# A two-layer decoder trunk in float32: layer B projects keys, queries, values in this order, with the norm gains in the weights, the branch shares in halves and the output projection in three passes

## The chip, the cores and the metric

The kernel runs on one NeuronCore of a Trainium2 chip. The metric is device time in microseconds (us) of one execution; before the change it was measured three times, with a median of 1330.33 us (1330.18 to 1332.09).

## The reference

The sequence has S = 512 tokens of D = 1024 channels, in float32; a head has 64 channels. Layer A is a sparse attention beside a memory attention, followed by a squared-relu MLP. Layer B, which the change is about, reads keys and values that are computed once from layer A's output. Cut to that part:

```
# layer A has left x; layer B:
k_s, v_s = split(rmsnorm(x, kv_norm) @ w_kv_shared, 2)      # 1024 -> 512 + 512, eight slots of 64
k = rope(rmsnorm(heads(k_s), kv_k_norm), pos);  v = heads(v_s)
h = rmsnorm(x, attn_norm[1])
q, q_mem = split(h @ b_w_in, [1536])                        # three groups of eight heads, four memory heads
q = rope(rmsnorm(q, b_q_norm), pos)
for gi, (window, dil) in enumerate(((128, 1), (512, 4), (2048, 16))):
    s = q[gi] . k[t - dil * j] / 8,  j = 0 .. window // dil # only t - dil * j >= 0
    lse[gi] = logsumexp(s);  out[gi] = softmax(s) . v
o_main = sum(out * softmax(lse over the three groups))
o_mem  = memory_attention(q_mem, mem_kv)                    # 256 memory rows, four heads
x = x + concat(o_main, o_mem) @ b_w_out                     # 768 -> 1024
x = x + squared_relu(rmsnorm(x, mlp_norm[1]) @ w_up) @ w_down
```

## The kernel before

**Number format.** Every float32 operand of a large product is kept as a high part, rounded to the format that TensorE reads, and a low part, the rest. A product is three matmuls: high by high, high by low, low by high (`mm3`, L232 to L234). For a weight, `wload` issues a DMA into a staging tile `s_st` (pool of three), ScalarE (ACT) writes the high part (`wsplit`, L225), and VectorE (DVE) or GpSimd (POOL) subtracts it for the low part (L227); the letters in `lo` choose between the two, "v" and "g". An activation is split in the same way; where a norm's gain belongs to it, `part` scales by the gain column while it splits (ACT L248, DVE L249).

**Order of the work.** The program is written as generators which are stepped against each other: `attend` walks through the attention items, and after each front (scores and exponentials) or back (the product with the values) it steps a side queue once and the list `work` as often as the ratio `RB` of that segment says. That fixes buffers and waits; a scheduler then orders the instructions of every engine by a model of their durations, so what stands on PE is not the program's order word for word. All weight loads are issued by SP's queue in order.

**Layer B** (L1351 to L1410). The transposed activations `xk`, multiplied by the gain of the K/V norm, come out of the end of layer A's MLP (`gained`, L1117, called at L1188). Keys are projected from w_kv[0] into the PSUM pool `pS` (blocks 2, 3, 0, 1), normalised and rotated, on POOL mostly (rope L483 to L486, L1381). Then the values are projected from w_kv[1]; each block of them is written to memory by a DMA that POOL issues (L1363), since `keys_b` reads them back in other row orders (L1464, L1466). Then 16 `gained` parts make `xg`, the same activations with layer B's own norm gain. Then the queries of slot pair 0 (`proj_b(0)`, 96 matmuls of 384 columns; evacuation L1424, ropes L483 to L486, L658, splits L617/L618, transposes on PE L667) are weaved with `keys_b(0)` (L1455 gathers, L1432). After step 34 of these, two steps of `work` follow each step.

`attn_b` makes eight items for each of four slot pairs: two halves of the tokens (`ih`), two slots (`s`), and `w` = 0 for the two groups with regular rows (window 128 and dilation 4), `w` = 1 for dilation 16 (scores L1492, exponentials L1522, transposes L1540 and L1549, value products L1562 and L1575). `close0` and `close1` take the sums out of PSUM. `norm_b` (L1584 to L1641) then merges the branches: it turns the statistics of `w` = 0 into the row order of `w` = 1 (L1589, L1595), works out the share of each branch (L1600 to L1615), transposes the shares (L1619), spreads them over the channels with two selection matmuls (L1627, L1632), multiplies (L1630, L1633), adds on POOL (L1634), and casts and splits on DVE (L1638, L1639). It begins in the side queue after `close1`, and `NY`, `NZ` are the steps that it lets pass in between. `work` holds the projections and keys of slot pairs 1 to 3, the memory queries and keys, and `outpart(0,2)`, the output projection of the first two chunks of the contraction, which adds its PSUM to the residual (L1084). After the last item, `outpart(2,6)` does the other four.

The names in the profile: `s_w` weights, `s_act` activations, `s_acc`, `s_ps`, `s_pt`, `s_po` the four PSUM pools (2, 3, 2 and 1 banks), `s_qk` split queries and keys, `s_qki` their split before the transposes, `s_tq` queries under way, `s_nb` the shares.

Of the kernel before, what the change touches and what calls it, by code (L numbers as in the profile page):

```python
# [47 lines left out]
RB = (1.58, 1.85, 1.49, 2.67, 1.4)  # L48
# [4 lines left out]
WK = 0.12  # L53
WB = (34, 2)

DELAY = 5

NY, NZ = 6, 2
# [107 lines left out]
class K:  # L166
# [105 lines left out]
    def proj(self, xg, wsrc, n, evac, blocks=NB, per=2, stat=None, banks=None, pool=None, lo="v", fine=False, hook=None, order=None):  # L272
# [259 lines left out]
    def mem_q(self, l, xg, wsrc, e, res):  # L532
# [13 lines left out]
        yield from self.proj(xg, wsrc, 256, evac, per=4, lo="gv")  # L546
# [513 lines left out]
    def outpart(self, oT, k0, k1, wsrc, xsrc, w0):  # L1060
# [56 lines left out]
    def gained(self, dst, m, h, gname):  # L1117

        H = S // 2
        self.part(dst[:, :, h * H : h * H + H], self.xh[h][m // 2][:, m % 2], self.gcol(gname)[:, m : m + 1])  # L1120

    def mlp(self, l):
# [43 lines left out]
        def columns(rows, cols):  # L1166

            for i in range(2):
# [8 lines left out]
                t = self.xh[rows][mp] = self.t("x", [P, 2, H])  # L1177
# [173 lines left out]
    def layer_b(self):  # L1351
# [412 lines left out]
```

## Time and profile before

| | |
|---|---|
| median of three runs | 1330.33 us |
| the profiled execution | 1332.11 us |
| its span, first to last instruction | 1330.3 us |
| mean granted TensorE clock | 0.982 |
| PE busy | 1272.9 us, 6425 instructions |
| DVE, ACT, POOL busy | 952.9, 765.9, 559.6 us |
| layer B up to its MLP | about 704 to 1000 us of the span |

The span is cut into stages by what runs there. From 704 to 764 us stand the projections of keys, values and the first queries; from 764 to 800 the second queries and the keys of pair 0; from 800 to 922 the attention of most pairs with the other projections; from 922 to 970 the last pair's end and the memory attention; from 970 the last part of the output projection. A row with "<-" and a releaser at its end names what the instruction waited for, and how long.

### The profile page before, as it was taken

The numbers are of one execution on the slowest core, as the hardware profiler recorded it, in microseconds if no ns is written. First come the engines' busy times: TensorE is split into PE (matmuls) and PEld (weight loads), VectorE is DVE, ScalarE is ACT, GpSimd is POOL, SyncE is SP. The second block draws the span as 40 slices with busy tenths as digits, with TensorE's granted clock in tenths as the row PEclk, the third lists the DMA queues.
The fourth block names the chain that finished last, engine by engine and source line by source line (L and its number), as shares of the span: only waits on it lengthen the run. The fifth ranks groups of instructions, "written<-read, shape, count | busy, mean of one in ns | idle before, by whom it ended". The sixth has DMA issues, their size and how long they took to land.

```text
span 1330.3 us, 18523 instructions
## 1 busy us (share of the span) xinstructions
PE 1272.9 (96%) x6425; PEld 1039.0 (78%) x6425; DVE 952.9 (72%) x1645; ACT 765.9 (58%) x1742; POOL 559.6 (42%) x578
## 2 busy tenths in 40 slices
PE   8999999999999999999999989989899999999997
PEld 6777787777787888888877879877578788888886
DVE  5877677764669678696798476676658967769586
ACT  5657577773465454554557557776655546355462
POOL 3765475442155041341415697452416324133140
PEclk9999899999999999999999999999899999999999
DMA  8313111023522525325244321012232342624423
GB/s 302 104 57 98 63 49 40 4 70 97 156 92 77 179 80 174 127 92 162 96 139 135 123 84 62 23 33 84 72 119 95 112 149 88 188 97 126 144 80 111
DMA packets 51534, 139.11 MB, mean 105 GB/s; under 512 B 5648, under 2 KB 12816, under 8 KB 51440
## 3 DMA queue, kind: packets, MB, share of 16 engines
q1 hardware_dynamic: 50224, 134.66, 32.3%
q0 software_dynamic: 640, 2.21, 0.5%
q8 instruction: 51, 0.84, 0.3%
q10 hardware_dynamic: 576, 1.05, 0.2%
q14 instruction: 43, 0.35, 0.1%
HBM read 132.66 MB, written 5.24 MB: 104 GB/s over the span
## 4 chain that ended last, share of the span: by engine, by line
PE 71%; DVE 16%; ACT 6%; issue 3%; DMA 3%; POOL 0%; DVEq 0%; ACTq 0%; POOLq 0%
PE s_ps L233 11%; PE s_ps L234 11%; PE s_ps L232 11%; DVE s_w L227 6%; PE s_acc L233 5%; PE s_acc L232 5%; PE s_acc L234 5%; DVE s_p L1104 3%; PE s_po L1045 3%; PE s_pt L232 2%; PE s_pt L233 2%; PE s_pt L234 2%; ACT s_w L225 2%; PE s_pt L1032 1%; PE s_ps L996 1%
## 5 line engine op out<-in xcount | busy, mean ns | idle before, releaser
L227 DVE TENSOR_TENSOR s_w<-s_st,s_w 128x1024 fp32r<-128x1024 f32 (+3 forms) x168 | 203.5, 1214 | 163.8 <-ACT s_w L225 163.1
L225 ACT ACTIVATE s_w<-s_st 128x1024 fp32r<-128x1024 f32 (+3 forms) x200 | 188.3, 946 | 157.3 <-PE s_pt L234 31.8
L232 PE MATMUL s_ps<-s_act,s_w 128*128 128x512 f32 x600 | 235.1, 393 | 2.0 <-ACT s_act L267 1.4
L233 PE MATMUL s_ps<-s_act,s_w 128*128 128x512 f32 x600 | 234.4, 391 | 0.0
L234 PE MATMUL s_ps<-s_act,s_w 128*128 128x512 f32 x600 | 234.1, 391 | 0.0
L1090 POOL TENSOR_TENSOR s_x<-s_x,s_st 128x512 f32<-128x512 f32 x64 | 102.0, 1611 | 90.3 <-DVE s_w L227 90.3
L232 PEld LDWEIGHTS s_ps<-s_act,s_w 128*128 128x128 f32 x600 | 112.4, 188 | 28.0 <-ACT s_act L267 3.1
L233 PEld LDWEIGHTS s_ps<-s_act,s_w 128*128 128x128 f32 x600 | 112.7, 188 | 24.2 <-issue 0.8
L234 PEld LDWEIGHTS s_ps<-s_act,s_w 128*128 128x128 f32 x600 | 112.7, 188 | 23.9 <-POOL s_p L642 0.8
L1090 POOL TENSOR_TENSOR s_x<-s_qki,s_st 128x512 f32<-128x512 f32 x16 | 25.2, 1573 | 214.5 <-DMA s_st<-in_w_db_dram 194.8
L232 PE MATMUL s_acc<-s_w,s_act 128*128 128x512 f32 (+2 forms) x272 | 99.6, 371 | 11.5 <-ACT s_w L225 5.5
L642 POOL TENSOR_SCALAR s_p<-s_p,s_cr 128x256 f32<-128x256 f32 (+3 forms) x128 | 71.9, 576 | 86.8 <-DVE s_cr L1008 25.5
L233 PE MATMUL s_acc<-s_w,s_act 128*128 128x512 f32 (+2 forms) x272 | 98.9, 364 | 0.1
L234 PE MATMUL s_acc<-s_w,s_act 128*128 128x512 f32 (+2 forms) x272 | 97.1, 361 | 0.0
L227 DVE TENSOR_TENSOR s_w<-s_x,s_w 128x512 fp32r<-128x512 f32 x96 | 90.5, 978 | 8.1 <-ACT s_w L225 8.1
L227 POOL TENSOR_TENSOR s_w<-s_st,s_w 128x512 fp32r<-128x512 f32 (+3 forms) x32 | 55.2, 1727 | 81.5 <-ACT s_w L225 62.7
L267 ACT ACTIVATE s_qk<-s_p 128x256 fp32r<-128x256 f32 (+1 forms) x96 | 47.0, 490 | 64.0 <-DVE s_p L1104 62.0
L1219 ACT ACTIVATE s_p<-s_ps 128x512 f32<-128x512 f32 x64 | 38.0, 593 | 79.3 <-PE s_ps L234 79.3
L270 DVE TENSOR_TENSOR s_qk<-s_p,s_qk 128x256 fp32r<-128x256 f32 (+1 forms) x96 | 76.9, 801 | 8.0 <-ACT s_qk L267 8.0
L225 ACT ACTIVATE s_w<-s_x 128x512 fp32r<-128x512 f32 x96 | 57.2, 623 | 38.1 <-POOL s_x L1090 38.1
L232 PEld LDWEIGHTS s_acc<-s_w,s_act 128*128 128x128 f32 x272 | 53.2, 196 | 17.8 <-ACT s_w L225 5.5
L1104 DVE TENSOR_TENSOR s_p<-s_p,s_p 128x256 f32<-128x256 f32 x96 | 59.5, 620 | 3.9 <-ACT s_p L1220 3.9
(347 smaller groups left out, 3218.4 us busy)
## 6 DMA issues: line engine op xcount, KB each, us to landing
s_st<-in_w_db_dram SPq DMA_DIRECT2D x80, 512.0 KB, 3.6
s_st<-in_w_up_dram SPq DMA_DIRECT2D x64, 512.0 KB, 3.7
s_st<-in_w_bq_dram SPq DMA_DIRECT2D x16, 384.0 KB, 3.2
s_st<-in_w_ag_dram SPq DMA_DIRECT2D x11, 512.0 KB, 4.4
s_act<-in_w_c_dram SPq DMA_DIRECT2D x8, 512.0 KB, 5.1
s_st<-in_w_mem_dram SPq DMA_DIRECT2D x8, 512.0 KB, 3.5
s_st<-in_w_ao_dram SPq DMA_DIRECT2D x16, 256.0 KB, 2.6
s_tq<-in_w_db_dram SPq DMA_DIRECT2D x16, 256.0 KB, 3.1
```

The source lines that it names most:

```text
L225: nc.scalar.activation(w[:, 0], st, AF.Copy)
L227: e.tensor_tensor(out=w[:, 1], in0=st, in1=w[:, 0], op=ALU.subtract)
L232: mm(ps, lh[0], rh[0], start=start, stop=False, skip_group_check=again)
L233: mm(ps, lh[0], rh[1], start=False, stop=False, skip_group_check=again)
L234: mm(ps, lh[1], rh[0], start=False, stop=stop, skip_group_check=again)
L267: nc.scalar.activation(dst[:, 0], src, AF.Copy)
L270: nc.vector.tensor_tensor(out=dst[:, 1], in0=src, in1=dst[:, 0], op=ALU.subtract)
L642: self.nc.gpsimd.tensor_scalar(out=p, in0=p, scalar1=c, scalar2=1.0, op0=ALU.mult, op1=ALU.mult)
L1045: nc.tensor.matmul(O[x * 64 : x * 64 + 64, q0 + o : q0 + 256], v[:, j, br, :], st[x][br][:, j, o:256], start=half == 0 and br == 0 and j = ...
L1090: self.nc.gpsimd.tensor_tensor(out=o, in0=x, in1=b[:, i * 512 : (i + 1) * 512], op=ALU.add)
L1104: tt = lambda o, x, y, op: nc.vector.tensor_tensor(out=o, in0=x, in1=y, op=op)
L1219: nc.scalar.activation(u, ps, AF.Relu)
```

## The change

The three-matmul products and the total of matmuls remain. These things change:

- `wload` takes gains. The rows of w_kv, w_bq and w_bm are multiplied by the norm gain while they are split: per k-chunk one scaled copy on ACT (L252) and one DVE instruction (L253), in place of one ACT copy and one subtraction, on DVE or POOL in turn, over the whole load. `gained` goes away: the end of layer A's MLP splits the plain activations, and one set of them serves keys, values and all queries.
- The order is keys, queries of pair 0, values. Of `proj_b(0)` all 36 steps of matmuls come first, into `pS`; then the values, into `pacc`, are weaved with its late steps and with `keys_b(0)`. `keys_b` waits for the fourth block of values before it reads them back. The interleaving after step 34 (`WB`) is gone.
- `norm_b` becomes three: `turned_b` enters the side queue after the last front of `w` = 0, `shares_b` after the last front of `w` = 1, and `join_b` runs inside `close1`. The sum moves from POOL to DVE, the copy from DVE to ACT (L1655).
- The output projection gets a third pass: `outpart(2,3)` joins `work`, on `pacc`, and the last is `outpart(3,6)`. It evacuates eight blocks more.
- The ratios RB rise for pairs 0 to 2.

```
-RB = (1.58, 1.85, 1.49, 2.67, 1.4)
+RB = (2.3, 2.3, 2.3, 2.67, 1.4)
-WK = 0.12
-WB = (34, 2)
+WK = 0.4
-NY, NZ = 6, 2
+NY, NZ = 1, 1
...
+        n = src.shape[-1] // gains.shape[1]
+        for j in range(gains.shape[1]):
+            c = slice(j * n, (j + 1) * n)
+            self.part(w[:, :, c], st[:, c], gains[:, j : j + 1])
...
-                    self.gained(self.xk[m], m, rows, "kv")
+                    self.split(self.xk[m][:, :, rows * H : rows * H + H], t[:, m % 2])
...
-        drain(self.proj(xk, ins["w_kv"][0], 512, evac_k, pool=self.pS, order=(2, 3, 0, 1)))
-        drain(self.proj(xk, ins["w_kv"][1], 512, evac_v, pool=self.pS))
-        xg = [self.t("act", [P, 2, S], F32R) for _ in range(KT)]
-        for m in range(KT):
-            for h in range(2):
-                self.gained(xg[m], m, h, "attn1")
...
+        work.add(self.outpart(oT, 2, 3, ins["w_bo"], None, 2, self.pacc))
+        drain(self.proj(xg, ins["w_kv"][0], 512, evac_k, pool=self.pS, order=(2, 3, 0, 1), gain="kv"))
+        q0, k0 = self.proj_b(0, xg, e, pb[0], self.pS), self.keys_b(0, kn, vd, kp[0])
+        v0 = self.proj(xg, ins["w_kv"][1], 512, evac_v, gain="kv")
+        for _ in range(NB * (KT + 1)):
+            next(q0)
+        drain(weave(v0, chain(q0, k0), WK))
...
-        drain(self.outpart(oT + om, 2, 6, ins["w_bo"], None, 2))
+        drain(self.outpart(oT + om, 3, 6, ins["w_bo"], None, 3))
...
+        while self.vrows < NB:
+            yield
...
+            if s == 1 and ih == 1:
+                side.add(self.shares_b(st1, s0, acc) if w else self.turned_b(st0, s0))
...
-            side.add(self.norm_b(st0, st1, acc[0], O, oT))
+            while len(acc) < 2:
+                side.step()
+            self.join_b(acc, O, oT)
...
-        nc.gpsimd.tensor_tensor(out=acc, in0=acc, in1=cb, op=ALU.add)
+        nc.vector.tensor_tensor(out=acc, in0=acc, in1=cb, op=ALU.add)
-        nc.vector.tensor_copy(nat(o[:, 0, :]), ap)
+        nc.scalar.activation(nat(o[:, 0, :]), ap, AF.Copy)
```

Since lines are inserted, later lines carry other numbers after the change: the matmuls L232 to L234 become L236 to L238, L225 becomes L229, L667 becomes L673, L564 and L577 become L570 and L583, L617, L624, L625 and L650 become L623, L630, L631 and L656, L1575 becomes L1579, L1619 becomes L1630.

**First place: PE, behind the queries of pair 0.** Before the change, PE's rows at the end of these queries (`s_ps`) are followed by the second queries (`s_acc`); the L667 rows are the transposes of the first ones:

```order
L233 MATMUL s_ps_7615<-s_w_7448,s_act_7382 128x384
L234 MATMUL s_ps_7615<-s_w_7448,s_act_7382 128x384
L232 MATMUL s_acc_7667<-s_w_7659,s_act_7375 128x384
L232 MATMUL s_acc_7746<-s_w_7659,s_act_7375 128x384
L667 MATMUL s_pt_7506<-idr,s_qki_7482 128x128 x4
L667 MATMUL s_pt_7513<-idr,s_qki_7482 128x128 x2
L233 MATMUL s_acc_7667<-s_w_7659,s_act_7375 128x384
```

After it, the same transposes (`s_pt_7345`) stand within the projection of the values (`s_acc`, 512 columns), 25 matmuls behind the end of the queries:

```order
L238 MATMUL s_acc_7517<-s_w_7512,s_act_6779 128x512
L237 MATMUL s_acc_7559<-s_w_7512,s_act_6779 128x512
L238 MATMUL s_acc_7559<-s_w_7512,s_act_6779 128x512
L236 MATMUL s_acc_7517<-s_w_7526,s_act_6830 128x512
L673 MATMUL s_pt_7345<-idr,s_qki_7326 128x128 x4
L673 MATMUL s_pt_7352<-idr,s_qki_7326 128x128 x2
L237 MATMUL s_acc_7517<-s_w_7526,s_act_6830 128x512
```

What moved: the 96 matmuls of the values, which stood ahead of the queries, now stand between their last matmul and their last transposes (94 of the 96 are ahead of these), and the second queries begin behind the values.

**Second place: ACT, at the memory keys of the end stage.** Before, two weight copies (L225) stand near the evacuations of the memory queries' transposes (L673) and keys (L624, L625):

```order
L225 ACTIVATE s_w_10087<-s_st_10085 128x512
L1567 ACTIVATE s_raw_9481<-s_po_9472 128x512
L650 ACTIVATE s_pt_2096_9535<-s_pt_9592 128x256
L650 ACTIVATE s_pt_2116_9628<-s_pt_9629 128x256
L673 ACTIVATE s_qk_9214<-s_pt_9633 128x2x128
L673 ACTIVATE s_qk_9215<-s_pt_9633 128x2x128
L617 ACTIVATE s_qki_9657<-s_tq_9655 128x4x64
L225 ACTIVATE s_w_10106<-s_st_10104 128x512
L624 ACTIVATE s_qk_9641<-s_pt_9647 64x4x128
```

After, there are six of them (L229) in the same stretch, most of 128x128, the third pass's:

```order
L656 ACTIVATE s_pt_2096_9584<-s_pt_9626 128x256
L229 ACTIVATE s_w_10057<-s_st_10055 128x128
L229 ACTIVATE s_w_10073<-s_st_10071 128x128
L656 ACTIVATE s_pt_2117_9679<-s_pt_9680 128x256
L229 ACTIVATE s_w_10083<-s_st_10081 128x128
L229 ACTIVATE s_w_10108<-s_st_10106 128x128
L679 ACTIVATE s_qk_9260<-s_pt_9691 128x2x128
L679 ACTIVATE s_qk_9261<-s_pt_9691 128x2x128
L623 ACTIVATE s_qki_9715<-s_tq_9713 128x4x64
L229 ACTIVATE s_w_10125<-s_st_10123 128x128
L229 ACTIVATE s_w_10149<-s_st_10147 128x384
L630 ACTIVATE s_qk_9699<-s_pt_9705 64x4x128
```

What moved: the copies for the third pass, each behind a DMA of its own, now stand in ACT's queue ahead of the evacuations.

**Third place: PE, the same stretch.** Before, no projection matmul stands between the transposes of the last pair and of the memory queries:

```order
L667 MATMUL s_pt_9633<-idr,s_qki_9610 128x128 x4
L564 MATMUL s_pt_9647<-idr,s_qki_9644 128x128 x4
L1575 MATMUL s_po_9699<-s_pt_2116_9628,s_x_9212 64x128
L1575 MATMUL s_po_9699<-s_pt_2096_9535,s_x_9212 64x128
L1575 MATMUL s_po_9699<-s_pt_2116_9628,s_x_9212 64x128
L1575 MATMUL s_po_9699<-s_pt_2096_9535,s_x_9212 64x128
L564 MATMUL s_pt_9660<-idr,s_qki_9657 128x128 x4
L1549 MATMUL s_pt_9695<-c_101,s_p_2115_9624 128x128 x2
L577 MATMUL s_ps_9677<-s_qk_9640,s_qk_9214 128x256
```

After, the third pass's matmuls (into `s_acc` of 128x512, one chunk of the contraction each time) stand among the same transposes (L673, L570), and the transposes of the shares (L1630) are already there:

```order
L238 MATMUL s_acc_10035<-s_act_9328,s_w_10032 128x512
L1630 MATMUL s_pt_9684<-idr,s_nb_9676 8x128 x4
L673 MATMUL s_pt_9691<-idr,s_qki_9644 128x128 x4
L236 MATMUL s_acc_10060<-s_act_9328,s_w_10057 128x512
L237 MATMUL s_acc_10060<-s_act_9328,s_w_10057 128x512
L238 MATMUL s_acc_10060<-s_act_9328,s_w_10057 128x512
L570 MATMUL s_pt_9705<-idr,s_qki_9702 128x128 x4
L236 MATMUL s_acc_10076<-s_act_9328,s_w_10073 128x512
L237 MATMUL s_acc_10076<-s_act_9328,s_w_10073 128x512
L238 MATMUL s_acc_10076<-s_act_9328,s_w_10073 128x512
L570 MATMUL s_pt_9718<-idr,s_qki_9715 128x128 x4
```

What moved: 24 matmuls that stood behind everything, in the last part of the output projection, now lie between the small steps of the last pair.

More of the change, by code (lines that the diff above doesn't have):

```diff
@@ L270, in split, with proj @@
         nc.vector.tensor_tensor(out=dst[:, 1], in0=src, in1=dst[:, 0], op=ALU.subtract)
-    def proj(self, xg, wsrc, n, evac, blocks=NB, per=2, stat=None, banks=None, pool=None, lo="v", fine=False, hook=None, order=None):
+    def proj(self, xg, wsrc, n, evac, blocks=NB, per=2, stat=None, banks=None, pool=None, lo="v", fine=False, hook=None, order=None, gain=None):
         ws = []
@@ L325, in proj @@
                     while len(ws) < min(nw, k // per + 2):
-                        ws.append(self.wload(wsrc[len(ws)], lo[len(ws) % len(lo)]))
+                        i = len(ws) * per
+                        gs = self.gcol(gain)[:, i : i + per] if gain else None
+                        ws.append(self.wload(wsrc[len(ws)], lo[len(ws) % len(lo)], gs))
                 if ps is None:
@@ L530, in mem_kv, with mem_q @@
         res.append(kf)
-    def mem_q(self, l, xg, wsrc, e, res):
+    def mem_q(self, l, xg, wsrc, e, res, gain=None):
         nc = self.nc
@@ L544, in evac @@
             return self.q_out(G, f, [q4[0][:, :, blk], q4[1][:, :, blk]])
-        yield from self.proj(xg, wsrc, 256, evac, per=4, lo="gv")
+        yield from self.proj(xg, wsrc, 256, evac, per=4, lo="gv", gain=gain)
         res.append(q4)
@@ L1132, in mlp @@
             self.xd = self.dram.tile([KT, P, S], F32, name="xd")
-            self.xk, self.xh = [None] * KT, [[None] * 4 for _ in range(2)]
+            self.xk = [None] * KT
             ss = self.c("ss", [P, 2, NB])
@@ L1176, in columns @@
                         )
-                t = self.xh[rows][mp] = self.t("x", [P, 2, H])
+                t = self.t("x", [P, 2, H])
                 if i:
@@ L1395, in layer_b @@
             work.add(self.keys_b(sp, kn, vd, kp[sp]), sp, lambda sp=sp: seen.count(sp - 1) == 8)
-        work.add(self.mem_q(1, xg, ins["w_bm"], e, qm))
+        work.add(self.mem_q(1, xg, ins["w_bm"], e, qm, "attn1"))
         work.add(self.mem_keys(1, self.kf1, kk), "mem")
         work.add(self.outpart(oT, 0, 2, ins["w_bo"], xd, 0))
-        first = weave(self.proj_b(0, xg, e, pb[0], self.pS), self.keys_b(0, kn, vd, kp[0]), WK)
-        for i, _ in enumerate(first):
-            for _ in range(WB[1] if i >= WB[0] else 0):
-                work.step()
+        work.add(self.outpart(oT, 2, 3, ins["w_bo"], None, 2, self.pacc))
[5 more added lines that the diff above has]
+        drain(weave(v0, chain(q0, k0), WK))
         items = []
@@ L1434, in evac @@
             return self.q_out(t, f, [q4[0][:, :, b * P : (b + 1) * P], permuted(q4[1]), permuted(q4[2])])
-        yield from self.proj(xg, ins["w_bq"][sp], 384, evac, pool=pool, lo="gv")
+        yield from self.proj(xg, ins["w_bq"][sp], 384, evac, pool=pool, gain="attn1")
         res.extend(q4)
@@ L1552, in back @@
                 close1()
-        acc = []
+        acc, s0 = [], []
         def close0():
@@ L1629, in norm_b, with join_b @@
         nc.scalar.activation(cb, pc, AF.Copy)
-        nc.vector.tensor_tensor(out=cb, in0=O1, in1=cb, op=ALU.mult)
         pc = self.ps(self.pT, [P, S])
         nc.tensor.matmul(pc, self.sel[:, 0, :], rows, start=True, stop=True)
-        nc.vector.tensor_tensor(out=acc, in0=acc, in1=pc, op=ALU.mult)
-        nc.gpsimd.tensor_tensor(out=acc, in0=acc, in1=cb, op=ALU.add)
+        nc.vector.tensor_tensor(out=acc[0], in0=acc[0], in1=pc, op=ALU.mult)
+        acc.append(cb)
+    def join_b(self, acc, O1, oT):
+        nc = self.nc
+        acc, cb = acc
+        nc.vector.tensor_tensor(out=cb, in0=O1, in1=cb, op=ALU.mult)
+        nc.vector.tensor_tensor(out=acc, in0=acc, in1=cb, op=ALU.add)
         o = self.t("act", [P, 2, S], F32R)
```

25 lines of the change are left out of this document (14 added, 11 removed).

## The prediction

> **What bounds the kernel now.** I read the page first: what is busy, over the whole span.
>
> ```profile
> span 1330.3 us, 18523 instructions
> PE 1272.9 (96%) x6425; PEld 1039.0 (78%) x6425; DVE 952.9 (72%) x1645; ACT 765.9 (58%) x1742; POOL 559.6 (42%) x578
> ```
>
> PE bounds it, and the number of matmuls stays. So the change can give only time in which PE is idle or at a lower clock, within the stages it touches. Next the table of windows over layer B: start:end, length, then busy time and (in brackets) instructions of PE, PEld, DVE, ACT, POOL, then PE's granted clock, the DMA share and GB/s.
>
> ```profile
> 684.00:704.00 20.00, 16.22 (x82) 12.67 (x83) 18.37 (x35) 15.26 (x34) 0.00 (x0) 1.00 0.80 253
> 704.00:764.00 60.00, 60.00 (x289) 52.51 (x288) 36.16 (x82) 34.46 (x89) 40.26 (x53) 1.00 0.38 118
> 764.00:800.00 36.00, 28.99 (x165) 27.73 (x164) 28.13 (x42) 19.11 (x58) 34.51 (x35) 0.91 0.27 88
> 800.00:922.00 122.00, 116.17 (x832) 102.49 (x831) 82.51 (x184) 89.13 (x297) 61.18 (x70) 0.99 0.16 47
> 922.00:970.00 48.00, 39.09 (x213) 26.29 (x211) 23.97 (x52) 27.98 (x81) 17.82 (x25) 0.86 0.21 61
> ```
>
> From 704 to 764 us (keys, values, queries of pair 0) PE is never idle. What can be had stands in three stages. A, 764 to 800: idle 36.00 − 28.99 = 7.0 us, and by the clock (1 − 0.91) × 36 = 3.2. B, 800 to 922: idle 5.8, clock 1.2. C, 922 to 970: idle 8.9, clock 0.14 × 48 = 6.7. Together 32.8 us. The waits of PE say what ends the idle time; first in A, then in C (line, what it waited for: us, times, longest).
>
> ```profile
> PE s_pt L667 <- DVE s_qki L618: 3.4, 2, 2.3
> PE s_acc L232 <- DVE s_tq L1424: 2.5, 1, 2.5
> PE s_pt L1455 <- ACT s_qk L1432: 0.6, 1, 0.6
> PE s_ps L1492 <- DVE s_qk L623: 0.5, 1, 0.5
> ```
>
> ```profile
> PE s_pt L1549 <- issue: 3.2, 1, 3.2
> PE s_pt L1632 <- ACT s_pt L650: 2.3, 1, 2.3
> PE s_pt L1619 <- DVE s_nb L270: 1.1, 1, 1.1
> ...
> PE s_pt L1549 <- ACT s_pt L650: 0.5, 1, 0.5
> PE s_pt L1627 <- DVE s_p L1623: 0.3, 1, 0.3
> ```
>
> In A half of it is the chain of the first queries: PE has ended their matmuls, and their ropes and splits aren't through. In C, 2.3 + 1.1 + 0.3 = 3.7 us is the branch shares (L1619, L1627, L1632). The 3.2 "issue" is resolved by the timelines of ACT and PE (start, length, engine):
>
> ```profile
> 940.32 0.63 ACT L225 ACTIVATE s_w<-s_st 128x512 fp32r<-128x512 f32 x1 [2.35 <-DMA s_st<-in_w_bo_dram]
> ```
>
> ```profile
> 942.27 0.66 PE L1549 MATMUL s_pt<-c,s_p 128*128 128x128 f32 x2 [3.19 <-issue]
> ```
>
> ```profile
> ACT s_w L225 <- DMA s_st<-in_w_bo_dram: 11.3, 7, 3.5
> ```
>
> ACT takes its instructions in order. It stood 2.35 us before a weight copy whose DMA had not landed, the evacuations behind it were late, and PE stood 3.19 us. The last row, from the waits of 680 to 1000 us, has seven such waits on w_bo, 11.3 us: 1.6 each.
>
> **Part 1: queries before values.** The rows of POOL and PE around the end of the first queries:
>
> ```profile
> 741.99 0.61 POOL L1381 TENSOR_TENSOR s_x<-s_x,s_r 128x256 f32<-128x256 f32 x1
> ...
> 757.56 1.00 POOL L483 TENSOR_TENSOR s_rb<-s_tq,c 128x384 f32<-128x384 f32 x1 [6.00 <-DVE s_tq L1424]
> 758.64 1.01 POOL L484 TENSOR_TENSOR s_tq<-s_tq,c 128x384 f32<-128x384 f32 x1
> 759.74 0.61 POOL L485 TENSOR_TENSOR s_tq<-s_tq,s_rb 128x192 f32<-128x192 f32 x1
> 760.30 0.60 POOL L486 TENSOR_TENSOR s_tq<-s_tq,s_rb 128x192 f32<-128x192 f32 x1
> 760.98 0.83 POOL L658 TENSOR_TENSOR s_tq<-s_tq,s_r 128x384 f32<-128x384 f32 x1
> ...
> 764.55 1.71 POOL L484 TENSOR_TENSOR s_tq<-s_tq,c 128x384 f32<-128x384 f32 x1
> ```
>
> ```profile
> 762.87 2.53 DVE L227 TENSOR_TENSOR s_w<-s_st,s_w 128x768 fp32r<-128x768 f32 x1 [1.49 <-ACT s_w L225]
> 765.33 1.34 DVE L618 TENSOR_TENSOR s_qki<-s_tq,s_qki 128x384 fp32r<-128x384 f32 x1
> ```
>
> ```profile
> 766.73 0.70 PE L667 MATMUL s_pt<-idr,s_qki 128*128 128x128 f32 x6 [2.34 <-DVE s_qki L618]
> ```
>
> POOL ends the keys' ropes at 742.6. One block of queries costs it 1.00 + 1.01 + 0.61 + 0.60 + 0.83 = 4.05 us, so four are done at 742.6 + 16.2 = 758.8, and with a split of 1.34 the last are ready for PE at about 760. The 289 matmuls of this stage took 60 us, 0.208 each; the 96 of the values, now behind the queries, last 20 us or more and end, as the three projections together, at 764. That is some 4 us of margin: the 3.4 us go, and the 0.6 on the keys, which get the same cover. What is late next: the second queries follow the values at once, with weights whose buffers come free only in the values' last block, and their PSUM waits on L1424. I let those 2.5 + 0.5 us stand. Of the clock's loss I count back the same share, 4.0/7.0 × 3.2 = 1.8. **A: 5.8 us.** The values' DMAs (L1363) move behind the ropes on POOL, and SP reads them back behind seven loads of w_bq, the last of which waits until the values' weights are used up, near 764; the first product that needs them, in the row of L1562, stood at 812 before, so even 20 us later hides.
>
> ```profile
> L1562 PE MATMUL s_po<-s_pt,s_x x64: 272/379/689, 812.1 to 934.3; 128*64 128x256 f32 x48, 128*64 128x128 f32 x16
> ```
>
> On the clock the trace and the Trainium skill differ. In its page "TensorE: Matmul & The Clock Gate", section "HAM oscillation — how this bites in real kernels", it says: "The abstract rule is "no PE-idle gaps >~3.4µs."" Here stage A was granted 0.91 with no wait over 2.5 us, and C 0.86 with none over 3.2, so the measurement decides that shorter gaps cost clock as well; by the rule alone the terms for the clock (here and in C) would not come back, and the sum would be about 5 us smaller.
>
> **Part 2: gains in the weights.** The groups of 680 to 1000 us by form (count | busy, mean ns):
>
> ```profile
> L227 DVE TENSOR_TENSOR s_w<-s_st,s_w 128x1024 fp32r<-128x1024 f32 x18 | 22.5, 1255 | 11.9 <-ACT s_w L225 11.7
> ...
> L227 POOL TENSOR_TENSOR s_w<-s_st,s_w 128x768 fp32r<-128x768 f32 x8 | 16.0, 1999 | 3.1 <-ACT s_w L225 3.1
> ...
> L249 DVE SCALAR_TENSOR_TENSOR s_act<-s_x,gv,s_act 128x256 fp32r<-128x256 f32 x32 | 14.8, 517 | 4.5 <-ACT s_act L248 4.5
> ...
> L227 DVE TENSOR_TENSOR s_w<-s_st,s_w 128x768 fp32r<-128x768 f32 x8 | 11.4, 1420 | 8.2 <-ACT s_w L225 8.2
> ...
> L249 DVE SCALAR_TENSOR_TENSOR s_act<-s_x,gv,s_act 128x512 fp32r<-128x512 f32 x8 | 6.8, 875 | 0.2 <-ACT s_act L248 0.2
> ...
> L1084 DVE TENSOR_TENSOR s_x<-s_ps,s_x 128x512 f32<-128x512 f32 x8 | 5.3, 683 | 0.8 <-PE s_ps L234 0.8
> L1634 POOL TENSOR_TENSOR s_raw<-s_raw,s_p 128x512 f32<-128x512 f32 x4 | 5.1, 1277 | 1.5 <-DVE s_cr L583 1.5
> ...
> L1638 DVE CAST s_act<-s_raw 128x512 fp32r<-128x512 f32 x4 | 4.1, 1026 | 5.0 <-POOL s_raw L1634 5.0
> ```
>
> Removed: the 16 parts for layer B's own gain, 16 × 0.517 = 8.3 us of DVE and about as much of ACT. They lay in 704 to 764, where PE is full: worth 0. Added: a piece of 384 columns lies between 0.517 (256) and 0.875 (512); I take the middle, 0.70. The 16 query loads become 32 × 0.70 = 22.4 us on DVE where 11.4 were, and POOL loses its 16.0. The memory queries: eight pieces of 256 columns, 4.1 where one 1.255 was: +2.9. A w_kv load becomes 2 × 0.875 = 1.75 for 1.255: +0.5, and four of the eight fall near the end of layer A's MLP, where DVE is busy 18.37 of 20. That can cost 0 to 2 us; I take **T: −1.0**, the middle, because PE is idle there for 3.8 us. POOL's relief frees nothing that PE waits for except the ropes.
>
> **Part 3: the shares by half, and the third pass.** Shares of `w` = 0 and 1 are worked out before the last value products, so the 3.7 us of C go. `join_b` puts 4 × 0.68 = 2.7 us on DVE (the size of L1084) and takes 4.1 of casts to ACT and 5.1 off POOL. The copy on ACT now waits for DVE's sum; behind it in ACT's queue stand evacuations (L656) for which PE waits, once a pair. The 24 matmuls of the third pass leave the last part and fall among the small steps of C; I let them fill half of the other 8.9 − 3.7 = 5.2 us, 2.6, and half the clock's 6.7 come back, 3.3. Against it stand eight more loads of w_bo in ACT's queue ahead of evacuations, 8 × 1.6 = 12.8 us of such waits if they wait like the seven before; those cost PE at least the 3.2 + 2.3 seen in C, about half of their 11.3, but DMAs of a quarter of the size land sooner. I take a quarter, −3.0 (0 to −6.4). **C: 3.7 + 2.6 + 3.3 − 3.0 = 6.6 us.** The third pass also evacuates eight more blocks, 8 × 0.683 = 5.5 us of DVE beside PE's work.
>
> **B.** The pairs' closing no longer stands in the side queue, and projections come sooner by RB. Nothing in the trace prices that. The bounds are plus or minus the stage's 5.8 us of idle time; I take a quarter, **+1.5**.
>
> **The sum.** 5.8 + 1.5 + 6.6 − 1.0 = 12.9 us. Against the profiled execution, 1332.1 us, that gives 1319.2; that execution is 1.8 above the median of the runs, so 1317.4. With C between 3.2 and 10 and B between −3 and +5, the likeliest case lies at 1309 to 1324.
>
> **Rivals.**
>
> R1, the end stage keeps its waits: ACT stands before the third pass's copies as it did before w_bo's, the full 6.4 us are paid, and the clock does not come back. C is then about −2 and the sum 5.8 + 1.5 − 1.0 − 2.0 = 4.3: 1326.0. For it speaks the row of 11.3 us; against it, that the pieces are small.
>
> R2, nearly all idle time closes: PE gets the third pass and the ropes in time everywhere, and 0.8 of the 32.8 us come back: 1304. Against it: the late L1424 waits have nothing that removes them.
>
> R3, the gap only moves: the second queries' weights, split on DVE alone while the values end, are late, and PE waits behind the values instead of behind the queries. A gives 0, B 0, C 3, T −1: 1328. For it speak PE's rows at the first queries:
>
> ```profile
> 763.35 0.33 PE L232 MATMUL s_ps<-s_w,s_act 128*128 128x384 f32 x1
> 763.53 0.33 PE L233 MATMUL s_ps<-s_w,s_act 128*128 128x384 f32 x1
> ```
>
> They start 0.18 us apart, so a block uses up a load's two chunks, six matmuls, in 1.1 us, while two pieces take DVE 1.40. It decides if PE's waits on the low parts are over 4 us.
>
> R4, slower: DVE becomes the bound of A and B. It gains 22.4 − 11.4 = 11.0 by query loads (a quarter of it before 764, so 8.2), 2.9, 2.7 − 4.1, and 5.5: 15.1 us on 28.13 + 82.51 + 23.97 = 134.6 of 206. In 764 to 800 it is busy for 78% already. The split at 762.87 took 2.53 against a mean of 1.42 while POOL ran ropes; twelve loads stretched by 1.1 are 13.3 more. If the 15.1 and half of the 13.3 reach PE, the result is 21.8 − 12.9 = 8.9 us slower: 1339. It decides where PE's waits on DVE exceed 12.9 us more than now. The Trainium skill ("SBUF — State Buffer", section "Who interferes with whom") says that a DVE instruction with two SBUF inputs contends with a GpSimd instruction that reads SBUF; the trace agrees (POOL's L484 took 1.71 beside that split, and 1.01 without).
>
> **How the numbers follow.** The likeliest case 0.45, R1 0.17, R2 0.10, R3 0.13, R4 0.15. About 0.2%, 2.7 us, can be told from no change: half of R3 lies within it. So faster 0.45 + 0.17 + 0.10 + 0.06 = 0.78, same 0.07, slower 0.15. The range runs from R2's 1303 to 1333, past R3; it leaves out R4 and a few hundredths at the lower end.
>
> **What would show it.** Right: no wait of L673 behind the first queries; the shares' L1630 and its matmuls without a wait in the end stage; A's and C's clock above 0.95. Wrong: PE waits on L253 at the second queries (R3) or all through 764 to 922 with DVE over 85% (R4); ACT before L229 on w_bo for more than 20 us (R1). If the idle time goes but the clock stays at 0.86 to 0.91, the terms for the clock were wrong.

## The result, and the profile after

The changed kernel takes 1320.99 us (median of four runs, 1318.36 to 1322.36), where the kernel before took 1330.68 beside it. The ratio is 0.9918, with a 95% interval of 0.9894 to 0.9943: 10.9 us faster by the ratio (7.6 to 14.1), where 12.9 were forecast. The medians themselves are 9.7 apart. In the experiments, below, the ratio was 0.9910 (0.9886 to 0.9933). Three executions among the experiments, of 1412.55, 2510.42 and 3181.12 us, far above the others of their kernels, are left out of every ratio and median. The profiled execution took 1319.75 us. Its page begins:

```profile
span 1317.5 us, 18596 instructions
PE 1270.7 (96%) x6425; PEld 1034.2 (78%) x6425; DVE 961.4 (73%) x1680; ACT 770.1 (58%) x1768; POOL 538.7 (41%) x569
```

The matmuls are as many as before; DVE has 8.5 us more and POOL 20.9 less. To compare stages, both spans have to be cut at the same work, not at the same time. I cut at the first matmul of the keys, the first of the second queries, the last of the fourth queries, the last of the memory queries, the first transpose of the memory attention, its last product, and the last transpose of layer B's second norm. The windows of the kernel before, cut there:

```profile
703.60:763.90 60.30, 60.30 (x291) 52.77 (x290) 36.46 (x83) 34.76 (x91) 40.16 (x53) 1.00 0.38 119
763.90:866.60 102.70, 94.46 (x611) 86.19 (x609) 69.78 (x124) 68.97 (x217) 74.55 (x79) 0.95 0.17 55
866.60:902.50 35.90, 31.30 (x258) 27.41 (x258) 26.31 (x60) 25.99 (x91) 18.35 (x22) 1.00 0.10 30
902.50:948.90 46.40, 39.73 (x247) 31.46 (x245) 28.97 (x64) 30.34 (x95) 11.32 (x15) 0.85 0.36 106
948.90:968.60 19.70, 18.16 (x92) 11.45 (x93) 9.53 (x29) 10.42 (x31) 9.40 (x16) 1.00 0.05 14
968.60:1007.00 38.40, 37.71 (x180) 30.30 (x179) 25.41 (x29) 25.22 (x41) 13.76 (x10) 1.00 0.40 130
```

And of the changed kernel:

```profile
701.80:767.40 65.60, 64.64 (x315) 55.54 (x313) 46.80 (x94) 36.74 (x104) 47.16 (x63) 0.98 0.30 97
767.40:857.90 90.50, 88.15 (x579) 80.30 (x577) 67.12 (x137) 63.14 (x199) 49.83 (x59) 0.98 0.25 72
857.90:896.40 38.50, 34.91 (x257) 29.78 (x257) 27.43 (x66) 30.16 (x103) 14.63 (x18) 0.91 0.10 28
896.40:946.30 49.90, 45.35 (x282) 33.56 (x280) 33.89 (x77) 32.89 (x107) 11.85 (x18) 1.00 0.33 97
946.30:963.60 17.30, 16.33 (x83) 9.89 (x82) 7.53 (x18) 11.46 (x36) 7.64 (x15) 1.00 0.08 24
963.60:999.20 35.60, 34.91 (x167) 28.14 (x166) 24.41 (x28) 25.03 (x40) 12.39 (x9) 1.00 0.45 139
```

The rows do not hold quite the same matmuls (the counts behind PE's busy time). The first stage is 5.3 us longer, since the first queries' transposes now lie in it, and the second 12.2 shorter: 6.9 together. The third and fourth are 2.6 and 3.5 longer, but the fourth holds the 24 matmuls of the third pass, whose place is missing in the last row (35.6 for 38.4); the fifth is 2.4 shorter. From the keys to the last row it is 303.4 − 297.4 = 6.0 us. The rest of the 12.8 by which the spans differ lies outside: 1.8 ahead of the first row, in work that the change leaves alone but for the last splits, and 5.0 behind the last, from layer B's end through its MLP. Of these 5.0, the last 130 us of the span hold 2.6 by the clock alone (0.98 before, 1.00 after), in work that the change does not touch. How much of the rest is scatter, two executions don't tell; the timed runs, 10.9 apart by the ratio, are the measure.

The stage that matters first is the start of the second queries. POOL's last rope of the first queries and PE's first transposes of them:

```profile
758.14 0.84 POOL L664 TENSOR_TENSOR s_tq<-s_tq,s_r 128x384 f32<-128x384 f32 x1
```

```profile
747.37 0.62 PE L673 MATMUL s_pt<-idr,s_qki 128*128 128x128 f32 x6
```

The ropes end at 759.0 (758.8 was forecast), and the transposes, the last of them at 765.71, follow within the values' matmuls with no bracket behind them: no wait. (91 of the 96 matmuls of the values, not 94, ran ahead of the last of them.) From 767.4 to 796 us PE has no wait at all. In the middle, 796 to 918, PE's longest waits are other ones than before:

```profile
PE s_pt L1630 <- ACT s_qk L1432: 2.0, 1, 2.0
PE s_pt L1455 <- ACT s_qk L1432: 1.6, 1, 1.6
PE s_pt L673 <- DVE s_p L1634: 0.8, 1, 0.8
```

L1630 is the transpose of the shares: it now waits here. From 896 to 946.3, the end, the gap of 3.2 us is gone, and of the waits on the shares 0.3 us is left (L1638, a selection matmul):

```profile
PE s_acc L236 <- DVE s_x L1090: 1.5, 4, 0.7
PE s_po L1579 <- ACT s_pt L656: 0.9, 2, 0.5
PE s_ps L1502 <- ACT s_p L1524: 0.8, 1, 0.8
...
PE s_pt L1638 <- ACT s_qk L631: 0.3, 1, 0.3
```

ACT's waits for w_bo's DMAs, from 680 to 1000 us, are more than the 11.3 of before, as the extra loads let expect; no wait of PE of over 1 us in this stage stands behind them:

```profile
ACT s_w L229 <- DMA s_st<-in_w_bo_dram: 12.6, 9, 3.0
```

### The profile page after: what moved, and what is told of

Its sections match the earlier page's. It is cut to its first block, busy times and chain, and to the rows that moved or that the text cites. A ratio compares the mean times of both kernels' runs of the same rounds, so it can differ in the third digit from the quotient of the medians.

```text
span 1317.5 us, 18596 instructions
## 1 busy us (share of the span) xinstructions
PE 1270.7 (96%) x6425; PEld 1034.2 (78%) x6425; DVE 961.4 (73%) x1680; ACT 770.1 (58%) x1768; POOL 538.7 (41%) x569
## 4 chain that ended last, share of the span: by engine, by line
PE 75%; DVE 13%; ACT 5%; DMA 3%; issue 2%; POOL 1%; SPq 0%; ACTq 0%; DVEq 0%; POOLq 0%
PE s_ps L237 11%; PE s_ps L236 11%; PE s_ps L238 11%; PE s_acc L236 6%; PE s_acc L237 6%; PE s_acc L238 6%; DVE s_w L231 5%; PE s_po L1051 3%; PE s_pt L238 2%; PE s_pt L237 2%; PE s_pt L236 2%; DVE s_p L1110 2%; PE s_ps L1002 1%; PE s_pt L1038 1%; DVE s_pt L1298 1%
## 5 line engine op out<-in xcount | busy, mean ns | idle before, releaser
L231 DVE TENSOR_TENSOR s_w<-s_st,s_w 128x1024 fp32r<-128x1024 f32 (+4 forms) x155 | 182.8, 1182 | 142.9 <-ACT s_w L229 142.1
L229 ACT ACTIVATE s_w<-s_st 128x1024 fp32r<-128x1024 f32 (+4 forms) x182 | 166.0, 917 | 143.0 <-PE s_pt L238 32.8
L236 PE MATMUL s_ps<-s_act,s_w 128*128 128x512 f32 x592 | 231.7, 393 | 1.8 <-ACT s_act L271 1.4
L238 PE MATMUL s_ps<-s_act,s_w 128*128 128x512 f32 x592 | 231.0, 391 | 0.0
L237 PE MATMUL s_ps<-s_act,s_w 128*128 128x512 f32 x592 | 231.0, 390 | 0.0
L236 PEld LDWEIGHTS s_ps<-s_act,s_w 128*128 128x128 f32 x592 | 111.0, 188 | 26.4 <-ACT s_act L271 3.1
L237 PEld LDWEIGHTS s_ps<-s_act,s_w 128*128 128x128 f32 x592 | 111.2, 188 | 23.8 <-issue 0.8
L238 PEld LDWEIGHTS s_ps<-s_act,s_w 128*128 128x128 f32 x592 | 111.1, 188 | 23.6 <-POOL s_p L648 0.8
L236 PE MATMUL s_acc<-s_w,s_act 128*128 128x512 f32 (+2 forms) x304 | 110.8, 370 | 8.5 <-ACT s_w L229 6.1
L237 PE MATMUL s_acc<-s_w,s_act 128*128 128x512 f32 (+2 forms) x304 | 111.2, 366 | 1.4 <-DVE s_w L253 1.0
L238 PE MATMUL s_acc<-s_w,s_act 128*128 128x512 f32 (+2 forms) x304 | 109.1, 363 | 0.0
L648 POOL TENSOR_SCALAR s_p<-s_p,s_cr 128x256 f32<-128x256 f32 (+3 forms) x128 | 71.6, 574 | 73.2 <-DVE s_cr L1014 24.5
L229 ACT ACTIVATE s_w<-s_x 128x512 fp32r<-128x512 f32 x96 | 57.4, 623 | 38.0 <-POOL s_x L1096 38.0
L231 POOL TENSOR_TENSOR s_w<-s_st,s_w 128x512 fp32r<-128x512 f32 (+4 forms) x27 | 37.6, 1398 | 97.2 <-ACT s_w L229 97.1
L236 PEld LDWEIGHTS s_acc<-s_w,s_act 128*128 128x128 f32 x304 | 59.0, 195 | 15.5 <-ACT s_w L229 6.1
L237 PEld LDWEIGHTS s_acc<-s_w,s_act 128*128 128x128 f32 x304 | 59.2, 195 | 8.7 <-DVE s_w L253 1.8
```

The costliest lines, as they stand in the source:

```text
L229: nc.scalar.activation(w[:, 0], st, AF.Copy)
L231: e.tensor_tensor(out=w[:, 1], in0=st, in1=w[:, 0], op=ALU.subtract)
L236: mm(ps, lh[0], rh[0], start=start, stop=False, skip_group_check=again)
L237: mm(ps, lh[0], rh[1], start=False, stop=False, skip_group_check=again)
L238: mm(ps, lh[1], rh[0], start=False, stop=stop, skip_group_check=again)
L648: self.nc.gpsimd.tensor_scalar(out=p, in0=p, scalar1=c, scalar2=1.0, op0=ALU.mult, op1=ALU.mult)
```

## Experiments

All were timed in turns with the kernel before on the same chip. A ratio is to the kernel before; 0.001 is 1.33 us. The theory is the sum of the prediction; the rivals are in each expectation. The number to compare with is the changed kernel's 0.991 to 0.992. First the changed kernel again.

> The changed kernel itself, so that the others of this call can be set against it on the same chip. Expected: 0.992 of the time before, 1321 to 1322 us where before takes 1332.

Measured: 0.9910 (0.9886 to 0.9933). It holds.

**The order undone.** In the changed kernel:

```
-        q0, k0 = self.proj_b(0, ...), self.keys_b(0, kn, vd, kp[0])
-        v0 = self.proj(xg, ins["w_kv"][1], 512, evac_v, gain="kv")
-        for _ in range(NB * (KT + 1)):
-            next(q0)
-        drain(weave(v0, chain(q0, k0), WK))
+        drain(self.proj(xg, ins["w_kv"][1], 512, evac_v, pool=self.pS, gain="kv"))
+        first = weave(self.proj_b(0, ...), self.keys_b(0, kn, vd, kp[0]), 0.12)
+        for i, _ in enumerate(first):
+            for _ in range(2 if i >= 34 else 0):
+                work.step()
```

> The changed kernel with the order undone alone: keys, values, then the queries of pair 0 weaved with their keys, as before; gains in the weights, shares by half, third pass and ratios stay. Theory (the sum of the prediction): the 5.8 us of stage A are lost again, so about 1327 us against the changed kernel's 1321.0, with PE waiting for the split of the first queries before their transposes (over 3 us) and a granted clock near 0.9 there. Rival (the ratios or the plain weights fill that gap whatever the order): within 2 us of 1321, no such wait.

Measured: 0.9951 (0.9933 to 0.9968), 1326.35 us: 0.0037 more than the mean of the changed kernel's two ratios, so 4.9 us of the gain are gone, with an interval of about 1.6 to 8.2. The theory (5.8) lies in it, and the rival (within 2 us) only at its edge. No usable trace was taken of this kernel, so the waits and the clock that were expected aren't shown by it.

**The order alone,** on the kernel before, with WK at 0.4 and the wait of `keys_b` for the fourth block of values:

```
-        drain(self.proj(xk, ins["w_kv"][1], 512, evac_v, pool=self.pS))
-        xg = [self.t("act", [P, 2, S], F32R) for _ in range(KT)]
-        for m in range(KT):
-            for h in range(2):
-                self.gained(xg[m], m, h, "attn1")
+        xg = xk
...
+        drain(self.proj(xk, ins["w_kv"][0], 512, evac_k, pool=self.pS, order=(2, 3, 0, 1)))
+        q0, k0 = self.proj_b(0, xg, e, pb[0], self.pS), self.keys_b(0, kn, vd, kp[0])
+        v0 = self.proj(xk, ins["w_kv"][1], 512, evac_v)
+        for _ in range(NB * (KT + 1)):
+            next(q0)
+        drain(weave(v0, chain(q0, k0), WK))
```

> The kernel before with the new order alone: keys, queries of pair 0, values weaved with their late steps and with the keys of pair 0. To make room for it, the 16 parts with layer B's own gain are left out, and the queries read the activations with the K/V gain, so a gain is wrong in them. Theory: the order alone gives stage A's 5.8 us, 0.9955 of before, with no wait before the first queries' transposes. Rival (without the higher ratios the gap moves behind the values, R3): 0.998 to 1.000, with PE waits over 3 us between 764 and 800 us.

Measured: 0.9937 (0.9914 to 0.9960), 8.4 us, more than the whole of the term. Its stage of the second to fourth queries is already as short as the changed kernel's, with the old ratios and the old weights, and PE has no wait from 764 to 800 us, so the rival (a gap behind the values) falls. The traced execution was 3.0 us below the median of this kernel:

```profile
767.70:858.70 91.00, 87.49 (x593) 79.82 (x592) 58.70 (x113) 63.60 (x200) 61.42 (x65) 1.00 0.24 75
```

**The 16 parts alone.** The edit above leaves them out, so they were measured by themselves, on the kernel before:

```
-        xg = [self.t("act", [P, 2, S], F32R) for _ in range(KT)]
-        for m in range(KT):
-            for h in range(2):
-                self.gained(xg[m], m, h, "attn1")
+        xg = xk
```

> The kernel before with nothing but the 16 parts with layer B's own gain left out; the queries read the activations with the K/V gain, so a gain is wrong in them. Theory (they lie under a full PE, worth 0): 0.9985 to 1.0015 of before. Rival (they stand on ACT and DVE ahead of the first queries' evacuations, and a good part of the 8 us measured for the new order with the parts left out is theirs): 0.997 or less, and the first queries' transposes no longer wait.

Measured: 0.9961 (0.9941 to 0.9981), 5.2 us. The theory, worth 0, falls; the rival holds by the time, but its wait shrinks and does not go. From 762.5 to 800 us, L667 has 1.2 us in place of 3.4 (L1421 is the L1424 of before):

```profile
PE s_acc L232 <- DVE s_tq L1421: 2.0, 1, 2.0
PE s_acc L233 <- DVE s_w L227: 1.2, 1, 1.2
PE s_pt L667 <- DVE s_qki L618: 1.2, 1, 1.2
```

The rows of ACT in the kernel before say where the parts were. Eight of the 16 could not run with the others, at 704: the pool of `s_act` has twelve tiles, the activations of keys and values hold eight, and these come free with the values' last matmuls; they stand at the start of the first queries, and the first evacuation of a query block (L464) comes 8.7 us after the queries' first matmul at 747.21:

```profile
742.65 1.71 ACT L248 ACTIVATE s_act<-s_x,gv 128x256 fp32r<-128x256 f32 x4
745.00 1.69 ACT L248 ACTIVATE s_act<-s_x,gv 128x256 fp32r<-128x256 f32 x4
...
755.92 0.49 ACT L464 ACTIVATE s_sq<-s_ps 128x384 f32<-128x384 f32 x1 [4.94 <-PE s_ps L234]
```

Without the parts the same row comes 7.7 us after the first matmul, and in the changed kernel 7.0. The row waited for PE (4.94 us), so late parts can delay it only through the matmuls that read them; PE was full here and took up other blocks meanwhile. This path is argued from the rows, and it is small in them: 1.0 us at the first evacuation, and PE's waits in this stage sum to 5.8 us without the parts and 7.0 with them, since one on a weight's low part (L233, 1.2) is new. The mean granted clock of the timed runs was 0.9845 without the parts and 0.9817 with them; time times one minus clock is 20.6 and 24.4 us, so up to 3.8 of the 5.2 may be the clock. The traced execution of this kernel was 3.9 us above its median, so it does not show where the rest is. Of the order's 8.4, then, some 3.2 are the order itself (0.9961 − 0.9937), though the intervals leave −1 to 7.

**The weights.** In the changed kernel:

```
-        yield from self.proj(xg, ins["w_bq"][sp], 384, evac, pool=pool, gain="attn1")
+        yield from self.proj(xg, ins["w_bq"][sp], 384, evac, pool=pool, lo="gv")
```

and the like for w_kv and w_bm.

> The changed kernel with the gains left out of w_kv, w_bq and w_bm: the weights are split whole, as before (low parts of w_bq and w_bm on POOL and DVE in turn), and no gain is applied at all in these projections. Theory: the split by chunks costs 1 us on the path (term T, near the end of layer A's MLP), the rest is hidden: about 1320. Rival (DVE is near the bound in 764 to 922 us, R4): DVE loses some 15 us of work and the kernel is 5 us or more faster, 1316 or less. Second rival (POOL's 16 us, taken off, were what the first queries' ropes needed): slower, 1323 or more.

Measured: 0.9907 (0.9884 to 0.9929): nothing that can be told from the changed kernel (0.9 us less, give or take 3.8), and neither rival fits. The splits with gains cost nothing that shows, though they are longer than I took them; the groups of the changed kernel, 680 to 1000 us:

```profile
L253 DVE SCALAR_TENSOR_TENSOR s_w<-s_st,gv,s_w 128x384 fp32r<-128x384 f32 x32 | 22.5, 745 | 5.9 <-ACT s_w L252 5.9
...
L253 DVE SCALAR_TENSOR_TENSOR s_w<-s_st,gv,s_w 128x512 fp32r<-128x512 f32 x16 | 15.7, 1020 | 2.0 <-ACT s_w L252 2.0
```

PE waited for them for 1.0 us in all from 680 to 1000 us:

```profile
PE s_acc L237 <- DVE s_w L253: 1.0, 2, 0.5
```

**The third pass undone.** In the changed kernel:

```
-        work.add(self.outpart(oT, 2, 3, ins["w_bo"], None, 2, self.pacc))
...
-        drain(self.outpart(oT + om, 3, 6, ins["w_bo"], None, 3))
+        drain(self.outpart(oT + om, 2, 6, ins["w_bo"], None, 2))
```

> The changed kernel with the output projection in two passes, chunks 0 and 1 in the list of work, 2 to 5 at the end. Theory: 2.6 us of filled gaps and half the clock's 6.7 us are lost, and 3.0 us of waits on w_bo saved: 1323 to 1325. Rival R1 (the copies behind the third pass's DMAs cost what it fills): 1319 to 1322, with ACT's waits on w_bo down from 12.6 to about 9 us and no longer PE gaps. Second rival (the third pass is most of the gain of the end stage): over 1326, with a gap over 3 us and a clock under 0.9 there.

Measured: 0.9960 (0.9939 to 0.9981), 1327.83 us: some 6 us worse than the changed kernel, with an interval of about 2.5 to 9.7. The second rival fits best, by time and clock, though its gap of over 3 us did not come; the theory's 1325 is not excluded. Its last three windows, against 49.90, 17.30 and 35.60, all at a clock of 1.00:

```profile
899.50:947.00 47.50, 40.85 (x250) 31.45 (x249) 27.97 (x65) 30.94 (x98) 9.56 (x12) 0.89 0.35 103
947.00:967.60 20.60, 20.32 (x100) 13.09 (x99) 7.57 (x18) 12.16 (x37) 7.92 (x16) 0.92 0.05 14
967.60:1006.00 38.40, 37.71 (x181) 30.32 (x179) 25.44 (x29) 25.26 (x41) 13.80 (x10) 1.00 0.42 131
```

24 matmuls are missing in the first of them (about 5.5 us at 0.23), and it is only 2.4 us shorter. PE's idle time is 47.50 − 40.85 = 6.7 us instead of 4.6, with one wait of 2.5 us for an evacuation by ACT, and the clock is 0.89. The other two windows, which take up 31 more matmuls, are 3.3 and 2.8 us longer, so the three together lose 3.7 us in this trace; the rest of the 6 is not in them:

```profile
PE s_po L1578 <- ACT s_pt L656: 2.5, 1, 2.5
```

ACT's waits on w_bo are fewer:

```profile
ACT s_w L229 <- DMA s_st<-in_w_bo_dram: 8.1, 7, 2.9
```

The changed kernel has 4.5 us more of them and is the faster one; no wait of PE of over 1 us stands behind them.

**The third pass alone,** on the kernel before:

```
+        work.add(self.outpart(oT, 2, 3, ins["w_bo"], None, 2, self.pacc))
...
-        drain(self.outpart(oT + om, 2, 6, ins["w_bo"], None, 2))
+        drain(self.outpart(oT + om, 3, 6, ins["w_bo"], None, 3))
```

> The kernel before with the third pass of the output projection alone. Theory (the third pass is the gain of the end stage, 5 to 6 us whatever stands before it): 0.995 to 0.997 of before, a granted clock over 0.95 in the end stage. Rival R1 (in the old order the copies behind its DMAs cost what it fills): 0.999 or more, with waits of ACT on w_bo well over 11.3 us and a PE gap behind them.

Measured: 0.9983 (0.9966 to 0.9999), 2.3 us: between theory and rival, and the interval touches both. ACT's waits on w_bo are 10.3 us, not over the 11.3 of before, so R1's sign is missing. It is less than the 6 in the changed kernel, but the two intervals overlap. The end stage of this kernel:

```profile
901.70:947.20 45.50, 42.30 (x272) 33.53 (x271) 31.50 (x75) 30.80 (x104) 12.24 (x19) 0.96 0.35 98
947.20:970.00 22.80, 20.16 (x84) 11.75 (x82) 11.13 (x30) 10.77 (x33) 10.59 (x16) 0.78 0.12 35
```

The pair's end is filled and its clock is 0.96, but the loss reappears in the memory attention behind it, at 0.78, with a wait of 2.0 us on the shares (L1620), which still come late in this kernel.

**The shares undone.** In the changed kernel, with the function and the steps of before:

```
-            if s == 1 and ih == 1:
-                side.add(self.shares_b(st1, s0, acc) if w else self.turned_b(st0, s0))
...
-            while len(acc) < 2:
-                side.step()
-            self.join_b(acc, O, oT)
+            side.add(self.norm_b(st0, st1, acc[0], O, oT))
```

> The changed kernel with the shares undone: the whole merge begins after the last value product of a pair, with the sum on POOL and the cast on DVE, and the old steps between; order, weights, third pass and ratios stay. Theory: the waits on the shares at the end (3.7 us) come back, with some clock: 1325 to 1328. Rival (the third pass's matmuls cover the shares wherever they stand): within 2 us of 1321.

Measured: 0.9891 (0.9867 to 0.9916). And a second time:

> The changed kernel with late shares in all pairs, a second time (first 0.9891 of before, against 0.9918 and 0.991 for the changed kernel and 0.9919 for late shares in three pairs). Theory (late shares are no worse than early ones, since the third pass covers them): 0.989 to 0.992. Rival (they are truly faster, and this version beats both kernels): 0.989 or less. Second rival (the prediction's 3.7 us for early shares was right, and the first measurement was scatter): 0.994 or more.

Measured: 0.9913 (0.9888 to 0.9937). In both the late shares are no worse; that they are faster is not shown. Two windows of the second say why they even out, the second to fourth queries (against 90.50) and the memory attention (against 17.30):

```profile
766.80:850.70 83.90, 82.35 (x547) 76.00 (x546) 58.38 (x122) 61.31 (x200) 48.21 (x57) 1.00 0.24 75
...
938.10:960.60 22.50, 18.94 (x83) 11.14 (x82) 11.29 (x30) 10.74 (x32) 10.74 (x16) 0.85 0.13 35
```

The first is 6.6 us shorter, with 32 matmuls fewer in it; the second, where the shares now fall, 5.2 longer. A kernel between the two has early shares in the last pair only:

```
-            if s == 1 and ih == 1:
+            if s == 1 and ih == 1 and sp == 3:
                 side.add(self.shares_b(st1, s0, acc) if w else self.turned_b(st0, s0))
...
+            if sp < 3:
+                side.add(self.norm_b(st0, st1, acc[0], O, oT))
+                return
```

> The changed kernel with the shares by half in the last slot pair alone; pairs 0 to 2 merge after their last value product, as before the change. The kernel with late shares in all pairs measured 0.9891 of before. Theory (early shares cost waits in the middle, on L1630, and help at the end, where nothing covers them): 0.987 to 0.988. Rival (at the end the third pass covers the shares wherever they stand): 0.989, as with all late. Second rival (the gain of late shares was scatter): 0.991 to 0.992, as the changed kernel.

Measured: 0.9919 (0.9898 to 0.9941): the second rival. Whether the shares come early or late, and in which pairs, makes no difference in this frame that these intervals, of some 3 us to each side, can show.

**The shares by half alone,** on the kernel before, with NY and NZ at 1:

```
+            if s == 1 and ih == 1:
+                side.add(self.shares_b(st1, s0, acc) if w else self.turned_b(st0, s0))
...
-            side.add(self.norm_b(st0, st1, acc[0], O, oT))
+            while len(acc) < 2:
+                side.step()
+            self.join_b(acc, O, oT)
```

> The kernel before with the shares by half alone (turned, shares and join as in the changed kernel, with its steps between), all else as before. Theory of the prediction: the 3.7 us of waits on the shares at the end go, 0.996 to 0.997 of before. Rival (the waits only move to the middle stage and to ACT's evacuations): 0.999 or more, the waits on the shares' lines in the trace about as large as before's, in other places.

Measured: 1.0053 (1.0032 to 1.0074), 7 us slower than before. Its time is on the rival's side (0.999 or more) and beyond what either named. The second window, against 102.70:

```profile
763.90:872.20 108.30, 97.50 (x621) 86.97 (x620) 74.11 (x137) 68.16 (x217) 72.96 (x78) 0.95 0.17 52
```

It is 5.6 us longer, with ten matmuls more, idle for 10.8 us instead of 8.2, and the first queries' waits still in it:

```profile
PE s_pt L667 <- DVE s_qki L618: 3.3, 2, 2.3
```

Why this edit costs 7 us here and nothing in the changed kernel was not settled. Two causes can be ruled out: the clock, since the mean of the timed runs is 0.9820 beside 0.9817 for the kernel before, and the old ratios by themselves, since the next kernel has them together with early shares.

**The ratios undone,** in the changed kernel:

```
-RB = (2.3, 2.3, 2.3, 2.67, 1.4)
+RB = (1.58, 1.85, 1.49, 2.67, 1.4)
```

> The changed kernel with the old ratios RB for pairs 0 to 2 (1.58, 1.85, 1.49). Theory (term B of the prediction): 1.5 us slower than the changed kernel, 0.993 of before. Rival (the ratios carry the stage of the second to fourth queries, 102.7 us before and 90.5 after): 5 us or more slower, 0.996 or more.

Measured: 0.9932 (0.9906 to 0.9959), 2 to 3 us, with an interval that also holds 0: it agrees with the 1.5. The rival's 0.996 lies just outside the interval of this ratio; 5 us against the changed kernel, whose ratio has an interval of its own, is not excluded.

## Why the prediction was right, and which steps were not

The forecast was 1317.4 in a range of 1303 to 1333, and 12.9 us of gain; measured were 10.9. The sign and the size came out of the likeliest case, but not every term, and that the sum came so near is in part luck: the parts' 5.2 that it put at 0 and the shares' 3.7 that did not come stand against each other.

**The order (A, 5.8): right, for part of the reason.** The first queries' chain was covered as worked out: ropes done at 759.0, no wait of L673. Undone it costs 4.9 (0.9951 − 0.9914, the mean of the changed kernel's two ratios), alone it brings about 3.2; both have intervals of 3 to 4 us to each side. The 3.0 us of waits that I let stand (L1424, and 0.5 on the keys) went too: between 767.4 and 796 PE waits for nothing.

**The 16 parts, "worth 0": wrong.** The step failed by its argument, that instructions under a full PE cost nothing. Leaving them out brought 5.2 us (2.5 to 7.9). Half of them came late, at the head of the chain that PE waited for, and the wait on L667 fell by 2.2 us without them; how the rest reached the time is not shown. The term missed is as large as the one for the order.

**The shares (3.7 of C): wrong.** Their waits left the end stage, as forecast, and came back in part in the middle on L1630 (2.0 us). Undone they cost nothing, alone they lose 7 us. I took a wait that is removed in one place as time gained, without asking what the same instructions push back where they now stand.

**The third pass (2.6, 3.3 of clock, −3.0 for DMAs): the doubt was wrong, the size is open.** By these it was to be worth 2.9; undone it costs some 6 (0.9960 − 0.9914 is 6.1, give or take 3.6), alone it brings 2.3 (0.1 to 4.5). Both intervals hold 2.9. The −3.0 rested on 12.8 us more of ACT's waits on w_bo; they were 1.3 more than before, and no wait of PE of over 1 us stands behind them. The clock of the end came back whole (0.85 to 1.00) instead of by half.

**T (−1.0) and the weights:** not to be told from 0, and R3 and R4 with them: PE's waits on L253 sum to 1.0 us, and DVE's extra work was hidden.

**B (+1.5):** the ratios' share is 2 to 3 us by one experiment with a wide interval. The stage itself is worse than forecast in the trace of the change: the third window is 2.6 us longer, at a clock of 0.91.

**The clock (5.1 in all): near in size by the traces, not in place.** By the windows of the two traces, length times one minus clock is 12.1 us before (102.7 × 0.05 + 46.4 × 0.15) and 6.6 after (65.6 × 0.02 + 90.5 × 0.02 + 38.5 × 0.09): 5.5 less. The end gave back 7.0 where 3.3 were counted, and the third window lost 3.5 that were not. Over the whole span, the mean granted clock of the timed runs was 0.9816 for the kernel before and 0.9884 for the changed one on the same chip; 1331.9 × 0.0184 = 24.5 and 1321.0 × 0.0116 = 15.3 are 9.2 us apart, where the medians differ by 10.9. These products are upper bounds, since a stretch at a low clock costs nothing while PE is idle, and those over the whole span count stages that the change does not touch. Without the third pass the mean clock is 0.9825 (on another chip, where the kernel before had 0.9815) and the product 23.2 us. So anything from a part to most of the gain may have come by way of the clock, and the runs don't say how much.

**Slips in the sums.** With C, B and T as given, the likeliest case runs from 1310.5 to 1325.3, not 1309 to 1324; R2 gives 1304, not 1303. R1's −2 for C is not worked out: with the full 6.4 and no clock, 3.7 + 2.6 − 6.4 is about 0, and without the shares' 3.7 it is −3.8. None of these changes where the result falls.

The rule of the page "TensorE: Matmul & The Clock Gate" of the Trainium skill, section "HAM oscillation — how this bites in real kernels" (no idle gaps over about 3.4 us), was set aside in the prediction for the measured clock, and the runs bear that out: without the third pass the longest wait in the fourth and fifth windows was 2.5 us, and their clock was 0.89 and 0.92 against 1.00.

What stays open: why the shares by half lose 7 us in the old frame, how the late parts' 5.2 us come about, and whether the third pass is worth 2 us or 6.

## What to carry to other kernels

Work that lies under a full engine is free only if nothing that this engine will wait for stands behind it: follow the queue of the engine that does it to the next thing due, and see when its buffers let it start. A wait that an edit takes away counts as time gained only when it is known where the moved instructions now wait. And when many small gaps are filled with matmuls that can be had from elsewhere, the filled time and the clock can come back together, as at the end here, so one should be costed with the other.

## What the runs showed of the hardware that was not expected

The time of the same program scatters together with its clock: 23 timed runs of the kernel before had granted clocks that went, on the whole, with the time, from 1327.10 us at 0.983 to 1337.85 at 0.978. Windows of the traces show whole stages at 0.78 to 0.91 in which PE's longest single wait was 2.0 to 3.2 us. A DVE split with a gain took 745 ns for 384 columns and 1020 for 512 from a staging tile, where the same instruction on an activation of 512 columns took 875 in the kernel before.
